# TensorE's merged order planned with measured durations, and a minimum stay on dense tiles

## The chip, the cores and the metric

One core of a Trainium2 chip runs the kernel. The metric is the device time of one execution in microseconds (us), lower is better; the kernel before takes 3297.18 us (median of 3 runs, 3290.95 to 3297.7).

## What is computed

One inference step of a two-layer hybrid decoder, for a prompt of 1024 positions and 8 decode rows. Cut to what matters:

```python
def hybrid_layer(x, ...):                       # D = 1024, 8 attention heads, 8 RWKV heads of 64
    p = x @ w_in                                # dense: in-projection
    att = dilated_attention(rope(q), rope(k), v)            # three patterns, merged
    z = token_shift(p[..., ATT_COLS:], ...)
    rw = rwkv7_time_mix(z)                      # a scan over positions: state S carried on
    x1 = layer_norm(ALPHA * x + concat(att, rw) @ w_out)    # dense: out-projection
    return layer_norm(ALPHA * x1 + square(relu(x1 @ w_ff_up)) @ w_ff_down)  # dense: feed-forward
```

Two layers run one after the other; the state of the RWKV scan, the keys and the decode rows are results too.

## The kernel before

Positions are split into two halves of 512, so the dense work is four passes (l, h): layer l, half h. A dense product is split into three matmuls (high*high, high*low, low*high parts in fp32r: L370, L371, L372), 128 output rows by 512 columns (half 0) or by 256 and 264 to 272 columns (half 1). The weights are loaded, split by ScalarE and VectorE (L343, L344) and used once per pass.

All the rest of TensorE's work is small: `stage1` and `stage2` of the RWKV scan in units of 256 positions (32 units in all), attention, the transposes of `post_stream`, and the decode rows (`decode`, and `kv_stream` for their attention). Most of it runs on tiles of the array smaller than 128x128: `pl` (L1189), `pT` and `pX` (L1283), `pPQ` (L1323), `pO` (L1340, L1345, L1359) and `pz` (L1366). Each unit of stage 2 is a chain of some 16 such blocks; between two of them VectorE or ScalarE takes the result out of PSUM and makes the next operand.

TensorE's order is written at build time by the class `Streams`. Six generators (`s2`, `s1`, `att`, `post`, `kv`, `dense`, in that priority) yield steps with a modelled cost on TensorE, a modelled latency until the stream's next step is ready (multiplied by `SLK`: 1.2 in a stream's first pass, 2.2 later) and a PSUM bank's hold time. `run` steps a model clock: the first stream in priority that is ready goes next, so that dense matmuls fill what is left. `ahead` holds a stream back that is far ahead of the dense one, by the shares of `WORK` done. The engine executes its instructions in exactly this order and waits where an operand is late.

The dense stream itself waits at four places for the other streams: `Mix.wait` before each out-projection, which asks for the last unit of stage 2, the attention and, for half 1, `dec` and `kv` of that pass. The last of the four is reached inside pass (1, 0), in group 5 of the feed-forward, just ahead of the column means of a layer norm (`lnc`, L711): all of pass (1, 1)'s small work has to stand ahead of it in TensorE's order. `decode` for layer 1 is a chain behind the transpose `pdv` (L1258): DMA out and in, then four rounds of loading a piece of the state, updating it on VectorE and GpSimd and storing it (L1654 to L1665), then a DMA out and in again (L1669, L1672) and three small blocks on TensorE, `pdy` (L1676), `pdm` (L1680) and `pdq` (L1685).

Five stretches of the program are named here by those waits: A, up to the first out-projection's wait; B, C and D, up to the second, third and fourth; E, the rest, in which only dense work is left.

Of the kernel before, what the change touches and what calls it, by code (L numbers as in the profile page):

```python
# [42 lines left out]
ALT0 = 2500  # L43
ALT1 = 4
WORK = {"s2": (73e3, 74e3, 73e3, 74e3), "s1": (38e3, 42e3, 42e3, 45e3), "att": (29e3, 49e3, 29e3, 49e3),
        "dense": (519e3, 536e3, 382e3, 394e3)}
SLK = (1.2, 2.2)
PACE = 2.0
LEAD = 0.25
# [95 lines left out]
class Streams:  # L145
# [5 lines left out]

    def __init__(self, depth):
        self.now = 0.0
        self.depth = depth
        self.hist = {b: [] for b in depth}
        self.streams = []
        self.times = {}
        self.cost = {}  # L160
        self.phase = {}
        self.work = {}

    def add(self, name, gen, slack=(1.0, 1.0)):
        self.streams.append([name, gen, 0.0, None, None, slack])
# [56 lines left out]
    def run(self):  # L222
        while self.streams:
            best = None
            main = self.ready(self.streams[-1])
            for s in self.streams:
                t = self.ready(s)
                if t is None:
                    continue
                if main is not None and main <= self.now and s is not self.streams[-1] and self.ahead(s):  # L230
                    continue
                if t <= self.now:
                    best = (t, s)
                    break
                if best is None or t < best[0]:
                    best = (t, s)
            assert best is not None, [s[0] for s in self.streams]
            self.now = max(self.now, best[0])
            self.step(best[1])


def bc(ap, dims):
# [5 lines left out]
def body(ctx, tc, I, O):  # L248
# [17 lines left out]
    def bank(tag, name):  # L266
        return ps.tile([128, 512], F32, tag=tag, bufs=BANKS[tag], name=name)
# [93 lines left out]
    def dense_steps(items, kts, xhh, xll, res):  # L361

        pts = [bank("d", "dps") for _ in items]
        last = len(kts) - 1
        for i, (wk, kt) in enumerate(kts):
            cost = 0
            for p, (w, m, c0, n) in zip(pts, items):
                wh, wl = w[wk // 4]
                hi, lo = xhh(kt, c0, n), xll(kt, c0, n)
                PE.matmul(p[:m, :n], wh[:, wk % 4, :m], hi, start=(i == 0), stop=False)  # L370
                PE.matmul(p[:m, :n], wh[:, wk % 4, :m], lo, start=False, stop=False)  # L371
                PE.matmul(p[:m, :n], wl[:, wk % 4, :m], hi, start=False, stop=(i == last))  # L372
                cost += 3 * (n / 2.4 + 2.5)
            if i < last:
                yield (cost, None, 0, None)
        res += pts
        res.append(cost)

    def dense(items, kts, xhh, xll, evac):

        res = []
        yield (0, None, 0, "d")
        yield from dense_steps(items, kts, xhh, xll, res)
        for it, p in zip(items, res):
            r = evac(it, p)
            if r is not None:
                yield r
        for i, it in enumerate(items):
            yield (res[-1] if i == 0 else 0, ("d", 900 + 500 * i), 0, None)
# [1468 lines left out]
```

## Time and profile before

| | |
|---|---|
| median of 3 runs | 3297.18 us |
| profiled execution, its own time | 3297.23 us |
| its span, first to last instruction | 3295.4 us |
| TensorE matmul busy | 3148.5 us, 96%, 24732 instructions |
| VectorE, ScalarE, GpSimd busy | 2065.4, 1449.2, 985.1 us |
| mean granted TensorE clock | 0.983 of full speed |

TensorE is the busiest engine by far. Matmuls overlap in the pipeline, so a matmul's duration is longer than its pitch: what counts is the distance from one start to the next. Time in which TensorE is not busy is a wait, and the granted clock tells how much of the busy time ran at half speed.

### The profile page before, as it was taken

Reading aid. Unit: us, or ns where it says so; the run is one execution under the profiler, and the core shown is the slowest. Engines: PE = TensorE matmul, PEld = TensorE weight load, DVE = VectorE, ACT = ScalarE, POOL = GpSimd, SP = SyncE. Lnnn points to the kernel's source line nnn. Section 1 sums busy time; section 2 is a strip of 40 time slices with the busy share of each in tenths; the row PEclk is TensorE's granted clock in tenths of the full one; section 3 lists DMA queues with packets and bytes.
Section 4 is the critical chain, followed back from the end, with each engine's and each line's share of the span. In section 5 each row is a group of like instructions: output and inputs, shape, how many; then the busy total and the mean of one; then the engine's idle time right before and its main releaser. Section 6 shows DMA issues by size and latency. Waiting matters only on the chain. (4 is left out here: it accounts for less than half of the span.)

```text
span 3295.4 us, 65986 instructions
## 1 busy us (share of the span) xinstructions
PE 3148.5 (96%) x24732; PEld 2656.9 (81%) x24732; DVE 2065.4 (63%) x4703; ACT 1449.2 (44%) x3266; POOL 985.1 (30%) x1841
## 2 busy tenths in 40 slices
PE   9899999999999999989999999999999999899998
PEld 6668887776777787778999998877766778899997
DVE  4566566865555575687655566568765564875556
ACT  4455344543443364454444346445543333543334
POOL 2452436522112234452221022545321201520012
PEclk9999999999999999999999999999999999999999
DMA  7544545334433355532333235553443433423332
GB/s 229 149 136 127 147 123 154 102 114 137 118 94 95 91 157 166 175 89 87 104 96 86 81 91 171 155 157 98 122 132 108 118 93 102 133 81 93 92 90 83
DMA packets 370502, 393.57 MB, mean 119 GB/s; under 512 B 145816, under 2 KB 223080, under 8 KB 370184
## 3 DMA queue, kind: packets, MB, share of 16 engines
q10 hardware_dynamic: 121152, 213.44, 21.9%
q1 hardware_dynamic: 249032, 175.93, 18.7%
q8 instruction: 195, 3.19, 0.4%
q14 instruction: 123, 1.01, 0.1%
HBM read 325.30 MB, written 63.97 MB: 118 GB/s over the span
## 5 line engine op out<-in xcount | busy, mean ns | idle before, releaser
L370 PE MATMUL dps<-xh,wh 128*128 128x256 f32 (+3 forms) x2984 | 991.9, 332 | 18.6 <-ACT wh L343 8.1
L371 PE MATMUL dps<-xl,wh 128*128 128x256 f32 (+3 forms) x2984 | 945.5, 317 | 7.8 <-DVE xl L762 6.3
L372 PE MATMUL dps<-xh,wl 128*128 128x256 f32 (+3 forms) x2984 | 944.0, 316 | 1.7 <-DVE wl L344 1.5
L343 ACT CAST wh<-wr 128x512 fp32r<-128x512 f32 (+1 forms) x772 | 475.3, 616 | 842.4 <-PE dps L371 780.1
L344 DVE TENSOR_TENSOR wl<-wr,wh 128x512 fp32r<-128x512 f32 (+1 forms) x772 | 578.1, 750 | 348.6 <-ACT wh L343 334.3
L370 PEld LDWEIGHTS dps<-xh,wh 128*128 128x128 f32 x2984 | 566.1, 190 | 90.8 <-issue 26.7
L371 PEld LDWEIGHTS dps<-xl,wh 128*128 128x128 f32 x2984 | 566.9, 190 | 42.3 <-DVE xl L762 9.8
L372 PEld LDWEIGHTS dps<-xh,wl 128*128 128x128 f32 x2984 | 566.3, 190 | 40.5 <-DVE wl L344 3.9
L370 PE MATMUL dps<-hh,wh 128*128 128x512 f32 (+2 forms) x1600 | 535.7, 335 | 5.0 <-DVE hh L944 3.6
L371 PE MATMUL dps<-hl,wh 128*128 128x512 f32 (+2 forms) x1600 | 512.7, 320 | 4.0 <-DVE hl L833 2.8
L372 PE MATMUL dps<-hh,wl 128*128 128x512 f32 (+2 forms) x1600 | 511.9, 320 | 0.0
L370 PEld LDWEIGHTS dps<-hh,wh 128*128 128x128 f32 x1600 | 303.6, 190 | 44.2 <-issue 17.9
L372 PEld LDWEIGHTS dps<-hh,wl 128*128 128x128 f32 x1600 | 303.9, 190 | 22.4
L371 PEld LDWEIGHTS dps<-hl,wh 128*128 128x128 f32 x1600 | 304.2, 190 | 22.1 <-DVE hl L833 3.8
L1212 POOL TENSOR_TENSOR tm<-BL,XB 32x15 f32<-32x15 f32 (+7 forms) x480 | 155.4, 324 | 491.6 <-DMA BL<-d_el 406.4
L976 DVE TENSOR_TENSOR t<-dps,t 128x256 f32<-128x256 f32 (+1 forms) x240 | 123.5, 515 | 161.5 <-PE dps L372 161.0
L1214 POOL TENSOR_TENSOR XB<-XB,tm 32x15 f32<-32x15 f32 (+7 forms) x480 | 157.9, 329 | 34.1
L729 POOL TENSOR_TENSOR ln<-ln,lsq 128x256 f32<-128x256 f32 (+1 forms) x112 | 93.4, 834 | 235.0 <-ACT lsq L727 232.0
L944 DVE CAST hh<-rl 128x256 fp32r<-128x256 f32 (+2 forms) x200 | 73.4, 367 | 99.2 <-ACT rl L943 95.9
L718 POOL TENSOR_TENSOR t<-t,ln 128x256 f32<-128x256 f32 (+1 forms) x32 | 28.0, 914 | 351.8 <-ACT ln L712 351.8
L942 ACT ACTIVATE rl<-dps 128x256 f32<-128x256 f32 (+2 forms) x200 | 88.4, 442 | 99.3 <-PE dps L372 87.4
L370 PE MATMUL dps<-hh,xh 128*128 128x256 f32 (+1 forms) x368 | 113.2, 307 | 15.4 <-DVE t L933 6.3
(345 smaller groups left out, 5072.0 us busy)
## 6 DMA issues: line engine op xcount, KB each, us to landing
wr<-in_w_ff_up ACTq DMA_DIRECT2D x272, 256.0 KB
wr<-in_w_ff_down ACTq DMA_DIRECT2D x256, 256.0 KB
wr<-in_w_in ACTq DMA_DIRECT2D x220, 256.0 KB
stg<-d_qkv SPq DMA_DIRECT2D x128, 128.0 KB
wr<-in_w_out ACTq DMA_DIRECT2D x64, 256.0 KB
z<-d_z SPq DMA_DIRECT2D x24, 384.0 KB
d_qkv<-qe SPq DMA_DIRECT2D x128, 64.0 KB
kvc<-in_cache_k SPq DMA_DIRECT2D x32, 256.0 KB
```

The costliest lines, as they stand in the source:

```text
L343: self.copies.append(A.copy(h[:, :, :m], w[:, :, :m]))
L344: V.tensor_tensor(lo[:, :, :m], w[:, :, :m], h.bitcast(F32)[:, :, :m], op=ALU.subtract)
L370: PE.matmul(p[:m, :n], wh[:, wk % 4, :m], hi, start=(i == 0), stop=False)
L371: PE.matmul(p[:m, :n], wh[:, wk % 4, :m], lo, start=False, stop=False)
L372: PE.matmul(p[:m, :n], wl[:, wk % 4, :m], hi, start=False, stop=(i == last))
L718: G.tensor_tensor(t, t, self.cm[:, c0:c0 + n], op=ALU.subtract)
L729: G.tensor_tensor(s2, s2, sq, op=ALU.add)
L942: A.activation(r, p[:, :n], AF.Relu)
L944: V.tensor_copy(hh[:, c0:c0 + n], r)
L976: V.tensor_tensor(to, p[:, :n], to, op=ALU.add)
L1212: G.tensor_tensor(tv, bc(BL[:, 17 * j + 1:17 * j + 2], [(1, m), (0, j + 1)]), bc(XB[:, 16 * j:16 * j + 1], [(0, m), (1, j + 1)]), op=ALU.mult)
L1214: G.tensor_tensor(xv, xv, tv, op=ALU.add)
```

## The change

The cost of a dense matmul of n columns in the model goes from n/2.4 + 2.5 ns to 0.447 n + 4 ns, and the dense entries of `WORK` go up by the same 8%. Each time the order comes back to the dense stream after a step of another stream that took TensorE time, the model clock goes on by `SWITCH` = 280 ns. From the point on at which the dense stream has entered its first out-projection, such a return also sets `stay`: for the next `RUN` = 3200 ns of the model clock the dense stream goes on as long as the model has it ready, whatever else is ready. No instruction is added or removed; the order of TensorE's instructions changes, and with it that of the other engines and of the DMA queues, which the scheduler derives.

```diff
-        "dense": (519e3, 536e3, 382e3, 394e3)}
+        "dense": (561e3, 580e3, 413e3, 427e3)}
+RUN = 3200
+SWITCH = 280
...
     def __init__(self, depth):
...
+        self.stay = 0.0
+        self.away = False
...
     def run(self):
         while self.streams:
             best = None
-            main = self.ready(self.streams[-1])
+            last = self.streams[-1]
+            main = self.ready(last)
+            free = main is not None and main <= self.now
+            if free and self.now < self.stay:
+                self.step(last)
+                continue
             for s in self.streams:
                 t = self.ready(s)
                 if t is None:
                     continue
-                if main is not None and main <= self.now and s is not self.streams[-1] and self.ahead(s):
+                if free and s is not last and self.ahead(s):
                     continue
...
             self.now = max(self.now, best[0])
-            self.step(best[1])
+            if best[1] is not last:
+                at = self.now
+                self.step(best[1])
+                self.away |= self.now > at
+                continue
+            if self.away:
+                self.away = False
+                self.now += SWITCH
+                if "dense" in self.phase:
+                    self.stay = self.now + RUN
+            self.step(last)
...
-                cost += 3 * (n / 2.4 + 2.5)
+                cost += 3 * (0.447 * n + 4)
```

Lines behind the change stand 20 further down in the changed kernel (L370 is L390 there).

TensorE, end of stretch D, in the order before: the decode block `pdq` (`cst` holds constants, `a` the decode rows) stands among the dense matmuls of the feed-forward.

```order
L371 MATMUL dps<-xl_90,wh 128x512
L372 MATMUL dps<-xh_88,wl 128x512
L1685 MATMUL pdq<-a,cst 128x32
L370 MATMUL dps<-xh_88,wh 128x512
L371 MATMUL dps<-xl_90,wh 128x512
```

Between `pdv` and `pdq` there are 339 dense matmuls, and 138 more between `pdq` and the first `lnc`. The same place in the changed order, from the last blocks of the last unit of stage 2 on:

```order
L1386 MATMUL pz<-cst,St 64x64 x2
L1399 MATMUL pzf<-cst,Zp 64x64 x2
L1400 MATMUL pzf<-gs,gup 128x8
L1407 MATMUL pgm<-y,cst 128x256
L1408 MATMUL pgm<-gs,gup 128x256
L1416 MATMUL pgv<-gq,cst 128x256
L1696 MATMUL pdy<-cst,dyr 128x8 x4
L1700 MATMUL pdm<-a,cst 128x32
L1705 MATMUL pdq<-a,cst 128x32
L731 MATMUL lnc<-t,onec 128x256 x2
L390 MATMUL dps<-xh_88,wh 128x512
```

Only 21 dense matmuls are left between `pdv` and `pdq`, all of them close behind `pdv`, and none between `pdq` and `lnc`: the end of unit 30, the whole of unit 31, the last attention and the decode blocks stand in one row without a dense matmul among them.

TensorE, stretch A, the second unit of stage 1, from `pl` to the transposes `pt` of the same unit, before:

```order
L1189 MATMUL pl_981<-AR,BK 128x128
L1189 MATMUL pl_982<-AR,BK 128x128
L370 MATMUL dps<-xh_88,wh 128x512
L371 MATMUL dps<-xl_90,wh 128x512
L372 MATMUL dps<-xh_88,wl 128x512
L370 MATMUL dps<-xh_89,wh 128x512
L371 MATMUL dps<-xl_91,wh 128x512
L372 MATMUL dps<-xh_89,wl 128x512
L1231 MATMUL pt_1051<-cst,BK 128x128 x4
```

and with the change:

```order
L1209 MATMUL pl_918<-AR,BK 128x128
L1209 MATMUL pl_919<-AR,BK 128x128
L390 MATMUL dps<-xh_89,wh 128x512
L391 MATMUL dps<-xl_91,wh 128x512
L392 MATMUL dps<-xh_89,wl 128x512
L1251 MATMUL pt_1013<-cst,BK 128x128 x4
```

Three dense matmuls stand between the two blocks where there were six.

Counted over the whole order, stretches of dense matmuls go from 762 to 581, and the times that TensorE comes from a 128x128 tile (dense or not) to a smaller one from 552 to 517: 125 to 139 in stretch A, 162 to 139 in B, 126 to 122 in C, 139 to 117 in D.

## Rows read from the trace of the kernel before

**Rows 1.** The page: busy time by engine, and TensorE's granted clock in 40 slices.

```profile
PE 3148.5 (96%) x24732; PEld 2656.9 (81%) x24732; DVE 2065.4 (63%) x4703; ACT 1449.2 (44%) x3266; POOL 985.1 (30%) x1841
...
PEclk9999999999999999999999999999999999999999
```

**Rows 2.** Windows A to E: stretch, length, busy by engine (instructions), PEclk, DMA share, GB/s.

```profile
0.00:499.00 499.00, 475.02 (x3929) 384.96 (x3931) 302.51 (x805) 239.05 (x560) 185.72 (x394) 0.99 0.52 152
499.00:1356.40 857.40, 819.59 (x5837) 636.13 (x5834) 531.82 (x1193) 372.35 (x837) 274.84 (x544) 0.98 0.43 124
1356.40:2168.60 812.20, 781.98 (x6870) 718.19 (x6869) 521.28 (x1214) 371.63 (x858) 246.63 (x458) 0.99 0.39 113
2168.60:2737.40 568.80, 546.91 (x4143) 413.43 (x4142) 366.46 (x851) 242.74 (x556) 162.37 (x319) 0.98 0.40 116
2737.40:3295.40 558.00, 524.98 (x3962) 504.22 (x3960) 343.34 (x642) 223.47 (x457) 115.52 (x129) 0.97 0.32 96
```

**Rows 3.** TensorE's waits, stretches B to D: who waited for whom, total us, times, longest.

```profile
PE pz L1366 <- DVE St L1361: 9.1, 4, 2.7
PE dps L370 <- DVE t L933: 6.3, 2, 4.5
...
PE pS L1552 <- DVE bv L1250: 0.2, 1, 0.2
```

**Rows 4.** Timeline of TensorE: start us, us, engine, line, operation, tiles, shape, count.

```profile
871.02 0.40 PE L372 MATMUL dps<-hh,wl 128*128 128x512 f32 x1
871.35 0.33 PE L1366 MATMUL pz<-cst,St 64*64 64x64 f32 x4
871.61 1.16 PE L1189 MATMUL pl<-AR,BK 64*128 64x128 f32 x16
...
873.04 0.39 PE L371 MATMUL dps<-hl,wh 128*128 128x512 f32 x1
...
1012.57 0.39 PE L372 MATMUL dps<-hh,wl 128*128 128x512 f32 x1
1012.89 1.16 PE L1189 MATMUL pl<-AR,BK 64*128 64x128 f32 x16
...
1014.32 0.40 PE L371 MATMUL dps<-xl,wh 128*128 128x512 f32 x1
1014.55 0.40 PE L372 MATMUL dps<-xh,wl 128*128 128x512 f32 x1
1014.88 0.33 PE L1366 MATMUL pz<-cst,St 64*64 64x64 f32 x4
...
1015.48 0.40 PE L371 MATMUL dps<-xl,wh 128*128 128x512 f32 x1
```

**Rows 5.** TensorE's waits, stretch A.

```profile
PE pO L1359 <- DVE Z L1368: 4.3, 2, 3.9
PE pt L1231 <- DVE LB L1194: 4.2, 2, 2.2
```

**Rows 6.** Source line L1194: count, duration ns min/median/max, first and last start.

```profile
L1194 DVE TENSOR_TENSOR LB<-pl,cst x128: 405/414/426, 64.1 to 2591.3; 128x256 f32<-128x256 f32 x128
```

**Rows 7.** Timeline of TensorE: decode of layer 0 (first row) and layer 1, and `lnc`.

```profile
1027.57 0.29 PE L1258 MATMUL pdv<-cst,dvt 128*40 128x128 f32 x1
...
2604.02 0.27 PE L1258 MATMUL pdv<-cst,dvt 128*40 128x128 f32 x1
...
2699.98 0.41 PE L1676 MATMUL pdy<-cst,dyr 8*128 8x8 f32 x4
...
2707.36 0.30 PE L1685 MATMUL pdq<-a,cst 128*128 128x32 f32 x2
...
2739.51 1.02 PE L711 MATMUL lnc<-t,onec 128*128 128x256 f32 x4
```

**Rows 8.** Source line L1672: the last DMA in of each layer's decode, first and last start.

```profile
L1672 SPq DMA_DIRECT2D dyr<-d_y x2: 297/300/302, 1100.1 to 2673.5; - x2
```

**Rows 9.** Timeline of VectorE: the first of four rounds of layer 1's decode.

```profile
2618.07 0.69 DVE L1655 TENSOR_TENSOR dt<-ST,DV 128x512 f32<-128x512 f32 x1 [3.10 <-DMA DV<-d_dec]
```

## The prediction

> **What bounds the kernel now.** I read the page first: TensorE is busy for 3148.5 of 3295.4 us, the next engine for 2065.4, and the clock row is nearly full everywhere [rows 1]. So the time is TensorE's work plus its waits plus what a lower clock costs; a change of order leaves the work itself as it is. Then the windows by stretch, to place the waits: length less busy is 24.0 us in A, 37.8 in B, 30.2 in C, 21.9 in D and 33.0 in E [rows 2], 147 in all. The clock column says what ran at half speed: (1 - 0.98) * 857 = 17 us lost in B, 0.01 * 812 = 8 in C, 0.02 * 569 = 11 in D, 36 together. Then the waits by name for B to D: 41 rows, of which [rows 3] shows the first two and the last; 37 us are waits of dense matmuls and of the layer norm's blocks, which the change does not aim at, and 52 us are waits of the small blocks, the largest of them `pz` for `St`: a chain step whose operand was not ready when its turn in the order came. The profiled execution took 3297.23 us, against a median of 3297.18, so a difference worked out on it is one on the median too; about 0.2%, 6.6 us, is what a measurement of this kernel can tell from no change.
>
> **The change, term by term.**
>
> *Fewer comings and goings.* In [rows 4] a matmul of 512 columns takes 0.23 us from start to start (1014.32 to 1014.55). Around `pz` alone, from the last dense start before it to the second one after it, it takes 1015.48 - 1014.55 = 0.93, less two pitches 0.46. Around `pl` alone it is 1014.32 - 1012.57 - 0.47 = 1.28. Around both in one row it is 873.04 - 871.02 - 0.47 = 1.55, where 0.46 + 1.28 = 1.74 would be the sum. So putting two blocks of small tiles side by side saves 0.19 us, not the 0.28 that the model now charges for each return. What counts by this is how often TensorE comes from a 128x128 tile to a smaller one: 35 times fewer, at 0.2 us 7 us saved; by stretch, A has 14 more (2.8 us lost) and B, C and D have 49 fewer (9.8 us gained; 7 that follow at the end of D are counted in). The ends are nothing and 181 stretches fewer at 0.2, 36 us, if every avoided return saved as much; I keep 7, since many of the blocks that now stand together are a small tile beside a full one, for which I take no saving.
>
> The Trainium skill, TensorEngine Tiling (Array Packing), Key Properties, says that changing the tiling mode, and not just the tile, drains TensorE. By it a row of `pz` (64*64) and `pl` (64*128) would drain as well between the two and save nothing, and the sum below would be 7 us higher. The rows contradict that for this pair by 0.19 us, and I follow the rows.
>
> *Chains in B to D.* By the order and the pitch, the TensorE work between a `pO` and the next `pz` goes from 2.2 to 2.8 us to 3.3 to 4.4 us, since the stay keeps dense matmuls there for 3.2 us; the longer links, some 3.6 to 4.3 us before, change little. A wait like `pz`'s, 9.1 us in 4 times and 2.7 at most [rows 3], is then mostly covered. The gain lies between 10 us, where new waits arise as more blocks end at once and VectorE has to serve them together, and all 52. I take 28, a little over half: the short links go, the long ones, DMA waits and attention stay in part. With them goes part of the 36 us of the clock; half of it stands behind waits of small blocks, and half of that is 9 us (ends 0 and 20).
>
> *Stretch A.* Here nothing stays, the slack is 1.2, and the model's time passes faster per dense matmul, so fewer of them stand between two steps: three instead of six between `pl` and `pt` in the second unit, 0.70 us instead of 1.40, and about 1.1 instead of 1.4 between `pO` and `pz`. Four operations `LB` of 0.41 us [rows 6] lie behind `pl`, and `pt` needs a bank that the first two free, 0.83 us: what was covered is now just short, and where VectorE comes late the whole difference is paid. `pt` and `pO` already waited 4.2 and 4.3 us in two places each [rows 5]. Stretch A has some 8 units with about 16 links; 0.3 us paid on a fifth of these 130 would be 8 us. I take 9 with the clock (ends 0, as median links keep a margin, and 26, when two thirds pay).
>
> *The end of stretch D.* This is the largest term. TensorE takes its instructions in order, and behind the last of the 21 dense matmuls that follow `pdv` the order holds only small blocks until `pdq`; then come `lnc` and the dense work. So nothing dense can run until layer 1's decode has come through. How long that takes is in the trace. `pdv` started at 2604.02 [rows 7], the first of four rounds at 2618.07 [rows 9], the last DMA in was issued at 2673.5 [rows 8]: 69.5 us of DMA and VectorE work, with no dependence on dense matmuls. In layer 0 it is 1100.1 - 1027.57 = 72.5 us [rows 7, 8]. With an estimate of 3.1 us for that DMA to land (VectorE sat idle that long for the one of `DV` [rows 9]) and those 2707.36 - 2699.98 = 7.4 us [rows 7], `pdq` comes 80 us behind `pdv`. Before, 339 dense matmuls stood in that gap, 339 * 0.233 = 79 us, and 138 more, 32 us, between `pdq` and `lnc` at 2739.51 [rows 7]: all of it covered, with 32 us to spare. Now 21 * 0.233 = 4.9 us of dense work and 2.6 of small blocks lie behind `pdv`, so TensorE is without dense work for 80 - 7.5 = 72 us. In it stand the small blocks themselves: before, `pdv` to `pdq` took 103.3 us, of which 79 were dense, so the blocks of units 30 and 31 and their waits are 24; without the waits, and with the attention and `pdo` blocks that now come here too, I count 20 us of work. 72 - 20 = 52 us of waiting, and 3 more for dense matmuls that restart at the half clock: 55 us lost. The ends are 42, where the decode's DMAs get through 10 us sooner with the queue to themselves and the second load of `DV` is not held as it was before 2618.07, and 65, where VectorE's queue, now with unit 31's steps between the rounds, holds the rounds up. Unit 31's own waits of before are part of the 28, since they now lie inside this hole.
>
> *Sum:* 55 + 2.8 + 9 - 9.8 - 28 - 9 = +20 us, 3297.2 + 20 = 3317 us. Stretch E has no small work and keeps its order.
>
> **The rivals.**
>
> *The chains repay it (faster).* If the longer distances take away nearly all waits of small blocks, 45 of 52 us and 18 of the clock's 36, while the decode comes through at its short end (44 us) and A pays 3 with its entries: 44 + 3 - 45 - 18 - 9.8 = -26, 3271 us. For it: the links that waited most are those that become longest. Against it: `pz`, the largest of these waits, is 9.1 of the 52 us, and much of the rest lies on links that change less. It decides from the point at which the gains in B to D pass 58 us together.
>
> *A draw.* Both at half way: the end of D at 47, B to D gaining 47: 3297 us, within 6 us of before. Nothing speaks against it but the sizes.
>
> *Bunching (slower still).* In a burst after each stay up to four streams issue at once; two PSUM banks serve stage 1, attention and the decode rows, and VectorE at 63% [rows 1] takes their results together. If the new waits eat the 28 and 9, and A pays 20: 55 + 2.8 + 20 - 9.8 = +68, but then part of the bunches hides in the end of D; I put it at 3355.
>
> *The change does little.* That the model's stay is cut short because the model sees no dense step ready is excluded by the order itself: 338 of the 581 stretches are now 3.2 to 4 us long by the pitch, where 51 of 762 were.
>
> **How the numbers follow.** Forecast, slower by 7 to 45 us: 0.48. Bunching 0.10. Draw 0.18. Faster 0.24. The time is that of the forecast, 3317 us. The range reaches from 3276, which takes in the nearer half of the faster rival, to just below the bunching case, 3348, and leaves out about a fifth. Faster by over 0.2%: 0.24; within: 0.18; slower: 0.58.
>
> **What would show it.** In the profile after: a hole in TensorE's busy row just ahead of `lnc` in pass (1, 0), some 70 us from the last dense matmul to `lnc`, with the clock at half level and `pdy`, `pdq` waiting for the decode's DMA; waits of `pz` in B to D cut to a third; waits of `pt` and `pO` in A longer or more of them; windows B and C shorter than 857 and 812 us, D longer than 569. It is wrong if the hole is under 40 us, if A grows by over 25 us, or if B and C together shrink by over 50.

## The result and the profile after

The changed kernel takes 3342.18 us (median of 4 runs, 3337.59 to 3348.74), before on the same chip 3297.44: ratio 1.0141, 95% interval 1.0119 to 1.0163, or 45 us slower. The forecast was +20 us: the sign is right and the time lies in the stated range, but the loss is more than twice as large. The profiled execution after has a span of 3341.0 us. Two executions far from all others, one of e2 (5785.66 us) and one of the kernel before beside e9 to e12 (6189.77 us), were slow ones and are in no ratio below.

The page after, the rows that answer to [rows 1]:

```profile
PE 3160.8 (95%) x24732; PEld 2675.8 (80%) x24732; DVE 2070.7 (62%) x4703; ACT 1446.7 (43%) x3266; POOL 979.1 (29%) x1841
...
PEclk9999999999999999999999999999999988999999
```

The same instructions, and two slices of lower clock near the end of stretch D. The windows A to E after, to be read beside [rows 2]:

```profile
0.00:562.70 562.70, 512.22 (x4236) 411.07 (x4237) 326.78 (x863) 257.90 (x607) 211.23 (x471) 0.96 0.48 142
562.70:1380.40 817.70, 790.11 (x5518) 620.80 (x5516) 514.76 (x1132) 353.05 (x788) 246.36 (x465) 0.98 0.43 125
1380.40:2186.60 806.20, 779.87 (x6848) 718.26 (x6845) 510.87 (x1199) 368.44 (x852) 244.00 (x457) 0.97 0.40 114
2186.60:2782.40 595.80, 553.97 (x4187) 422.52 (x4186) 373.72 (x867) 244.37 (x563) 163.22 (x321) 0.95 0.39 113
2782.40:3341.00 558.60, 524.62 (x3954) 503.15 (x3953) 344.54 (x645) 222.95 (x458) 114.27 (x129) 0.97 0.32 95
```

A is 64 us longer, B 40 shorter, C 6 shorter, D 25 longer (cut as here, at the first `lnc`, it was 571 us). A part of A and B is only moved work: A has 4236 matmuls where it had 3929, B has 5518 where it had 5837. The waits are more than moved: in A, length less busy goes from 24.0 us to 50.5, at a clock of 0.96 in place of 0.99, while B's goes down by 10; in D it goes from 21.9 to 41.8, at 0.95.

TensorE's waits in stretch A after (who waited for whom, total us, times, longest):

```profile
PE pS L1583 <- POOL kS L1545: 9.3, 2, 6.7
PE dps L390 <- ACT wh L363: 6.6, 2, 5.3
PE pz L1386 <- DVE St L1381: 5.9, 2, 5.6
PE pO L1360 <- DVE Pt L1346: 4.3, 1, 4.3
PE pT L1303 <- DMA X<-d_el: 4.2, 3, 2.4
PE pET L1606 <- DVE E L1595: 3.4, 1, 3.4
```

Of these six, only two stood among A's waits before: `dps`, with the same 5.3 us at the start of the program, and `pz` for `St`, with 0.5 us. The new waits are few and long, not many and short. The chain behind the one of 4.3 us stands in the timeline after (start us, us, engine, line, operation; in brackets the idle time before it and what ended it):

```profile
404.29 1.09 ACT L1540 CAST qS<-stg 128x512 fp32r<-128x512 f32 x1 [5.39 <-DMA stg<-d_qkv]
...
405.28 0.61 ACT L363 CAST wh<-wr 128x512 fp32r<-128x512 f32 x1
...
405.93 1.59 DVE L364 TENSOR_TENSOR wl<-wr,wh 128x512 fp32r<-128x512 f32 x1 [3.33 <-ACT wh L363]
407.44 0.41 DVE L1346 COPY Pt<-pPQ 128x256 f32<-128x256 f32 x1
...
407.91 0.65 PE L1360 MATMUL pO<-LB,Pt 64*64 64x128 f32 x8 [4.31 <-DVE Pt L1346]
```

ScalarE sits for 5.39 us on the load of the attention's `stg` (it makes `qS` from it); the split of a dense weight (`wh`) is queued behind that, VectorE's half of the split (`wl`) waits for `wh`, and `Pt`, the operand of the scan, is queued behind `wl`. Three engines stop for one load. The waits of `pS` (`kS` is made from `stg`, and stands in GpSimd's queue as well) and `pET` lead back to `stg` too: with `pO` 17.0 us of A's waits.

The end of D after, timeline of TensorE, then the window of the hole:

```profile
2718.25 0.29 PE L1278 MATMUL pdv<-cst,dvt 128*40 128x128 f32 x1
...
2725.62 0.40 PE L392 MATMUL dps<-hh,wl 128*128 128x512 f32 x1
...
2779.93 0.59 PE L1696 MATMUL pdy<-cst,dyr 8*128 8x8 f32 x4 [2.57 <-DMA dyr<-d_y]
...
2781.98 0.64 PE L1705 MATMUL pdq<-a,cst 128*128 128x32 f32 x2 [0.54 <-ACT a L1702]
2782.43 2.05 PE L731 MATMUL lnc<-t,onec 128*128 128x256 f32 x4
```

```profile
2725.60:2782.40 56.80, 30.16 (x283) 20.07 (x282) 31.18 (x68) 8.13 (x23) 9.78 (x8) 0.59 0.33 95
```

The hole is there, from the last dense matmul to `lnc`: 56.8 us, 30.2 of them busy at a clock of 0.59.

**An account of the 45 us.** For each profiled execution I take, up to the last instruction, TensorE's idle time, half of its busy time at the half clock (1.2 of 2.4 GHz), and the dense matmuls at their pitch (0.233 us for 512 columns, as in [rows 4]); what is left over is the small blocks with all that coming and going costs. From before to after: idle time 136.0 to 169.3, clock 47.7 to 77.3, small blocks 857.6 to 840.3: +33, +30 and -17. (The level of 857.6 hangs on the pitch taken for the dense matmuls; the difference does not.)

### The profile page after: what moved, and what is told of

Its sections match the earlier page's. It is cut to its first block, busy times and chain, and to the rows that moved or that the text cites. A ratio compares the mean times of both kernels' runs of the same rounds, so it can differ in the third digit from the quotient of the medians.

```text
span 3341.0 us, 66018 instructions
## 1 busy us (share of the span) xinstructions
PE 3160.8 (95%) x24732; PEld 2675.8 (80%) x24732; DVE 2070.7 (62%) x4703; ACT 1446.7 (43%) x3266; POOL 979.1 (29%) x1841
## 5 line engine op out<-in xcount | busy, mean ns | idle before, releaser
L390 PE MATMUL dps<-xh,wh 128*128 128x256 f32 (+3 forms) x2984 | 985.9, 330 | 22.6 <-ACT xh L781 8.0
L390 PEld LDWEIGHTS dps<-xh,wh 128*128 128x128 f32 x2984 | 568.5, 191 | 93.4 <-issue 26.1
L390 PE MATMUL dps<-hh,wh 128*128 128x512 f32 (+2 forms) x1600 | 528.3, 330 | 5.2 <-DVE hh L964 3.6
L390 PEld LDWEIGHTS dps<-hh,wh 128*128 128x128 f32 x1600 | 304.9, 191 | 39.2 <-issue 11.3
L1232 POOL TENSOR_TENSOR tm<-BL,XB 32x15 f32<-32x15 f32 (+7 forms) x480 | 147.5, 307 | 571.1 <-DMA BL<-d_el 513.4
L390 PE MATMUL dps<-hh,xh 128*128 128x256 f32 (+1 forms) x368 | 110.0, 299 | 8.6 <-DVE t L1029 4.3
```

Source lines behind the costliest of these rows:

```text
L1232: G.tensor_tensor(tv, bc(BL[:, 17 * j + 1:17 * j + 2], [(1, m), (0, j + 1)]), bc(XB[:, 16 * j:16 * j + 1], [(0, m), (1, j + 1)]), op=ALU.mult)
```

## The experiments

A link is one step of a chain: the operand that VectorE or ScalarE makes, and the TensorE work that the order puts into that time. Its distance is that work; a link is too short when the next block's turn comes before its operand. Theory 1, before the first runs: the loss has two places, stretch A, where the charge makes the links too short at a slack of 1.2, and the hole at the end of D, which the stay opens. Its rivals: the bunching by the stay; the queue order of the other engines or the work moved into A, given back there; later, that any order other than that of before loses, whichever way the distances go.

Idle time of TensorE and length of the stretches, in us (cut at the same dense matmuls in all; for before within 3 us of [rows 2]), and the ratio to before. A loss in us is, from here on, that ratio applied to before's time on the same chip; for the changed kernel it gives +46.

| kernel | A | B | C | D | ratio, 95% |
|---|---|---|---|---|---|
| before | 24 of 498 | 38 of 858 | 30 of 812 | 22 of 571 | |
| after | 51 of 563 | 28 of 818 | 26 of 806 | 42 of 596 | 1.0141 (1.0119 to 1.0163) |
| e1 costs only | 27 of 510 | 49 of 873 | 31 of 815 | 21 of 563 | 1.0064 (1.0049 to 1.0079) |
| e2 costs, charge | 50 of 568 | 40 of 849 | 41 of 840 | 40 of 567 | 1.0255 (1.0236 to 1.0274) |
| e3 stay only | 24 of 497 | 47 of 849 | 25 of 807 | 46 of 605 | 1.0071 (1.0056 to 1.0086) |
| e4 after, no stay in D | 51 of 564 | 26 of 815 | 25 of 803 | 38 of 603 | 1.0137 (1.0114 to 1.0160) |
| e5 before, slack 0.85 in A | 53 of 554 | 29 of 842 | 30 of 816 | 21 of 569 | 1.0100 (1.0085 to 1.0115) |
| e6 after, charge late | 30 of 518 | 42 of 855 | 31 of 814 | 42 of 595 | 1.0118 (1.0101 to 1.0134) |
| e7 after, slack 1.6 in A | 30 of 518 | 43 of 853 | 31 of 814 | 46 of 597 | 1.0100 (1.0085 to 1.0115) |
| e8 stay only, not in D | 27 of 499 | 45 of 850 | 27 of 810 | 29 of 587 | 0.9993 (0.9982 to 1.0004) |
| e9 before, slack 1.5 in A | 24 of 479 | 40 of 882 | 30 of 809 | 23 of 577 | 1.0003 (0.9988 to 1.0017) |
| e10 before, slack 2.45 later | 25 of 498 | 43 of 869 | 24 of 807 | 27 of 580 | 1.0032 (1.0018 to 1.0046) |
| e11 before, slack 1.7 later | 26 of 512 | 46 of 871 | 26 of 823 | 29 of 550 | 1.0066 (1.0044 to 1.0088) |
| e12 costs, slacks raised | 29 of 502 | 38 of 862 | 25 of 805 | 27 of 586 | 1.0026 (1.0009 to 1.0043) |
| e13 after, stay ends in D | 52 of 565 | 27 of 819 | 27 of 806 | 25 of 575 | 1.0065 (1.0049 to 1.0080) |
| e14 e13 with slack 1.6 | 29 of 513 | 39 of 849 | 30 of 812 | 25 of 572 | 1.0031 (1.0017 to 1.0045) |
| e15 stay only, ends in D | 24 of 496 | 47 of 851 | 24 of 805 | 28 of 586 | 1.0002 (0.9990 to 1.0014) |
| e16 stay of 1600 only | 28 of 503 | 41 of 859 | 30 of 812 | 27 of 577 | 1.0019 (1.0009 to 1.0029) |
| e17 old costs, charge late | 26 of 502 | 41 of 848 | 37 of 823 | 19 of 574 | 1.0039 (1.0024 to 1.0053) |
| e18 stay only, slack 2.0 | 29 of 504 | 48 of 863 | 24 of 794 | 30 of 590 | 1.0035 (1.0022 to 1.0048) |

### The parts of the change alone (e1, e2, e3)

e1, the costs alone:

```diff
-SWITCH = 280
+SWITCH = 0
...
-                if "dense" in self.phase:
-                    self.stay = self.now + RUN
```

> Only the dense costs (0.447 n + 4 ns and the 8% in WORK); no charge per return, no stay. Theory 1 (the loss has two places: the 280 ns charge in stretch A, where the slack is 1.2, and the hole that the stay opens at the end of D): neither is here, A stays at 499 us within 12, between pdv and pdq 321 dense matmuls stand, so no hole; 3290 to 3310 us. Theory 2 (the costs themselves shorten the distances in A, since the model's time passes 8% faster per dense matmul): A grows by 20 us or more, 3315 us or more.

Measured +21 us (3317.28). The time lies in theory 2's range, A (12 us longer) in theory 1's; what neither had is B, 15 us longer, with 12 us more waits. A reading of this is that the old durations, 8% too low, had given each link 8% of distance for nothing; e12 below bears it out for 12 of the 21 us.

e2, the costs and the charge (only the two lines on `stay` taken out):

> Costs and the 280 ns charge per return, no stay. Theory 1: A comes out as in the changed kernel, 563 us within 8 with some 50 us of idle TensorE, and D has no hole (276 dense matmuls between pdv and pdq); the charge shortens the links in B to D too, where the slack of 2.2 leaves room; 3320 to 3345 us. Rival (bunching by the stay is what costs, the charge alone is harmless): 3290 to 3305 us, A within 10 us of 499.

Measured +84 us (3381.53, the median of the three executions that count), more than either theory. A is that of the changed kernel, as theory 1 has it; C is 28 us longer than before and D waits 18 us more, which I had not expected under a slack of 2.2. The windows A, B and C of this kernel:

```profile
0.00:568.10 568.10, 517.84 (x4236) 415.40 (x4237) 328.18 (x863) 258.59 (x607) 211.21 (x471) 0.95 0.48 140
568.10:1417.10 849.00, 809.04 (x5656) 633.63 (x5654) 525.05 (x1159) 366.64 (x816) 256.95 (x474) 0.98 0.44 124
1417.10:2257.00 839.90, 798.49 (x7037) 726.05 (x7034) 529.56 (x1254) 376.20 (x873) 246.38 (x458) 0.97 0.39 110
```

In the changed kernel the stay gives the distance back: B and C wait 28 and 26 us there, 40 and 41 here. So the charge costs 63 us more than the costs, and the stay repays 38 of that.

e3, the stay alone:

```diff
-        "dense": (561e3, 580e3, 413e3, 427e3)}
+        "dense": (519e3, 536e3, 382e3, 394e3)}
-SWITCH = 280
+SWITCH = 0
...
-                cost += 3 * (0.447 * n + 4)
+                cost += 3 * (n / 2.4 + 2.5)
```

> Only the stay of 3200 ns, with the old costs and no charge. Stretch A's order is that of before up to the first out-projection. Theory 1: A 499 us within 5; between the last pdv and pdq there is no dense matmul at all, so the hole ahead of lnc is there, 55 to 65 us long, 40 of it lost; B and C gain 10 to 20 us; in all 3310 to 3330 us. Rival (the loss of the changed kernel is the charge's, in every stretch, and the stay repays its hole by the chains in B to D): 3285 to 3300 us. Bunching: B and C grow, 3335 us or more.

Measured +23 us (3319.51): theory 1, but with a longer hole. A as before, B and C 14 us shorter, D 34 longer with a hole of 80.9 us (expected 55 to 65), 44.7 us of it lost: 32.3 idle and 12.4 of clock. B alone waits more than before, 47 us in place of 38.

This run also bears on what a return costs. 170 stretches of dense matmuls fewer than before (592 of 762) go with small blocks 16.3 us shorter (857.6 to 841.3), e16's 80 fewer with 7.4 us, the changed kernel's 181 fewer with 17.3: 0.10, 0.09 and 0.10 us each, where the model charges 0.28. It is an average, not a price: the other kernels with a stay give 0.07 to 0.16 us each, and e10, with 56 stretches more than before, has its small blocks 1.3 us shorter, not longer. Counted instead by the tiles in the traces' rows, TensorE comes from a 128*128 tile to a smaller one 63, 27 and 63 times less in e3, e16 and the changed kernel, and 0.26 to 0.28 us for each of these fits as well.

### Stretch A (e5, e6, e7, e9)

e5, the kernel before with shorter links in A by another route:

```diff
-SLK = (1.2, 2.2)
+SLK = (0.85, 2.2)
```

> The kernel before with one number changed: the first pass's slack 0.85 in place of 1.2, no charge, no stay, old costs. In stretch A as many dense matmuls then stand between pl and pt (median 3 in place of 6), pO and pz (mean 5.6, before 8.1) and pgm and pgv (9.4, before 15.9) as in the changed kernel or fewer. Theory 1 (A's loss is that small blocks' turns come before their operands): A grows like the changed kernel's, 545 to 580 us with 45 to 60 us of idle TensorE, and the total 3325 to 3350 us. Rival (A's loss is the queue order of the other engines that the charge brings, or the small work that moves from B into A and is given back there): A within 20 us of 498 apart from moved work, total within 10 us of before.

Measured +33 us (3336.34), A 554 us with 52.7 idle: theory 1. Windows A and B of this run, and its longest wait of a small block in A, the same as after:

```profile
0.00:554.00 554.00, 501.35 (x4087) 402.16 (x4088) 311.17 (x831) 251.70 (x588) 197.46 (x434) 0.96 0.50 141
554.00:1395.70 841.70, 812.88 (x5677) 634.99 (x5677) 518.78 (x1169) 365.61 (x810) 255.98 (x505) 0.97 0.44 124
```

```profile
PE pS L1563 <- POOL kS L1525: 8.3, 2, 5.0
```

B waits 28.8 us here, before 37.8, with no stay in this kernel: part of B's small work has moved into A (matmuls in A from 3929 to 4087, in B from 5837 to 5677), as it has in the changed kernel.

e9 goes the other way (`SLK = (1.5, 2.2)` in the kernel before):

> The kernel before with the first pass's slack 1.5 in place of 1.2, the opposite of the run with 0.85: in stretch A more dense matmuls stand between pT and pX (mean 12.4, before 9.6) and pO and pz (9.8, before 8.1). Theory 1 (distance: a small block that comes too early waits): A's waits do not grow, 24 us or fewer, A 490 to 500 us, total 3285 to 3300 us. Rival (any other order loses: the operands that come late are those that a queue of VectorE, ScalarE or GpSimd happens to hold up, in each order others): A 510 us or more, total 3310 us or more.

Measured +1 us (3303.03, 3 us above theory 1's range; before on that chip 3300.75), A's waits 23.6 us: longer links cost nothing there, though they gain nothing either. A is shorter than expected, 479 us, because small work moved to B. How ScalarE waits for `stg` in A follows the distance. Before, after, and e9 (total us, times, longest):

```profile
ACT kS L1524 <- DMA stg<-d_qkv: 18.5, 8, 4.7
ACT qS L1520 <- DMA stg<-d_qkv: 6.3, 4, 2.4
```

```profile
ACT qS L1540 <- DMA stg<-d_qkv: 16.6, 9, 5.4
ACT kS L1544 <- DMA stg<-d_qkv: 15.8, 8, 7.6
```

```profile
ACT kS L1524 <- DMA stg<-d_qkv: 9.9, 7, 2.6
ACT qS L1520 <- DMA stg<-d_qkv: 2.4, 2, 2.2
```

24.8, 32.4 and 12.3 us; with e5 it is 35.3. TensorE waits no less in e9 than before, though, so ScalarE's waits are not themselves the price. As I read it, before they lay under dense work, and with short links a step of the scan stands behind them, as in the chain shown above.

e6 charges the 280 ns only once `"dense" in self.phase`; e7 raises the slack of the changed kernel's first pass (`SLK = (1.6, 2.2)`).

> The changed kernel, but the 280 ns are charged only from the first out-projection on; in A only the higher costs are left. Theory 1: A comes back to 505 to 515 us, B takes some of the moved work back and is 825 to 850 us, C and D stay as in the changed kernel (D with its hole); 3305 to 3325 us. Rival (what A loses is gained in B): 3335 us or more.

> The changed kernel with 1.6 in place of 1.2 as the first pass's slack: the links of A have their dense matmuls back (pl to pt 6, pT to pX 10), with the charge kept. Theory 1: waits of A back to 24 to 32 us, A 500 to 520 us, total 3300 to 3320 us. Rival (the charge's order of the other engines is at fault, not the distance): A stays at 545 us or more.

Both have A back at 518 us with 30 idle, near theory 1 (e6's A is just above its range), but the totals are +39 and +33, above theory 1's ranges; e6, at 3339.91, is on its rival's side, by which what A loses is gained in B. B waits 42 and 43 us where the changed kernel waits 28. Of the 45 us that A comes back, 35 to 37 return in B, as the work that had moved into A and as waits. Net, A and B together are 1356 us before, 1380 after, and 1372 and 1371 here: repairing A is worth 8 to 13 us, not the 45 that A alone shows. The hole in these two kernels:

```profile
2724.90:2781.50 56.60, 30.19 (x284) 20.13 (x282) 31.24 (x68) 8.10 (x23) 9.78 (x8) 0.59 0.35 93
```

```profile
2722.20:2781.60 59.40, 28.81 (x299) 19.45 (x298) 31.18 (x69) 7.99 (x23) 9.78 (x8) 0.69 0.38 100
```

Outside it, B to D wait 88 and 90 us, and before 90: with A repaired, the changed kernel waits no less there than the kernel before.

### The end of stretch D (e3, e4, e8, e13, e15)

e4, the changed kernel without the stay in D:

```diff
-                if "dense" in self.phase:
+                if self.phase.get("dense", (2,))[0] != 2:
```

> The changed kernel, but without the stay while the third out-projection's pass is running (stretch D); 291 dense matmuls stand between pdv and pdq. Theory 1: the hole goes, and with it its 40 us of lost busy time and its half clock, while A keeps its loss: 3300 to 3315 us, D 555 to 570 us. Rival (the hole's time comes back as waits of unit 30's and 31's links spread over D): 3330 us or more, D 585 or more with as much idle TensorE as in the changed kernel.

Measured +45 us (3339.66), the rival's side. There is no hole, and D waits 38 us, nearly as long as with it (42). The first rows of its waits in D:

```profile
PE pT L1303 <- DMA X<-d_el: 6.6, 2, 5.8
PE dps L391 <- DVE xl L782: 6.5, 4, 3.4
PE pS L1572 <- DVE dT L1280: 4.9, 1, 4.9
```

The longest of them (5.8, 4.9 and 3.4 us) lie between 2316 and 2355 us, in the first third of D, some 370 us ahead of where the hole was. The edit changed the order of all of D, so this run did not test the hole. e8 makes the same edit to e3, e13 to e15 the cleaner one, which keeps D's order up to unit 29:

```diff
-                if "dense" in self.phase:
+                if "dense" in self.phase and (self.phase["dense"][0] != 2 or self.share("dense") < 0.5):
```

> Only the stay, with the old costs and no charge, and not while stretch D runs; 342 dense matmuls stand between pdv and pdq, so there is no hole. Theory 1, corrected by the run without the stay in D: A 497, B 849 and C 807 us as with the stay alone; D is 571 us within 10 if its loss there was the hole, so 3275 to 3290 us, faster than before. Rival (D loses by single late operands wherever its order is changed, as the run without the stay in D showed 38 us of idle TensorE without a hole): D 590 us or more, 3305 us or more.

> The changed kernel, but the stay ends when half of stretch D's dense work is done; 267 dense matmuls then stand between pdv and pdq (21 in the changed kernel), and the order up to unit 29 is that of the changed kernel. If the hole's 39 us of idle time and half clock are its own: D 570 to 582 us, total 3315 to 3330 us. Rival (unit 30's and 31's links find late operands wherever they stand): D 590 us or more, 3335 us or more.

> Only the stay, old costs, no charge, and it ends when two fifths of stretch D's dense work are done; 168 dense matmuls stand between pdv and pdq, so half of the hole is left at most. A and B 1345, C 807 as with the stay alone; D 575 to 588 us if the hole goes with its cover (605 with the stay throughout): 3285 to 3302 us. Rival (new late operands in D): D 595 or more, 3310 us or more.

Windows of stretch D, one after the other: with the stay (e3), e4, e8 and e13:

```profile
2152.70:2757.60 604.90, 558.98 (x4232) 426.66 (x4232) 371.67 (x871) 247.76 (x569) 164.29 (x320) 0.96 0.39 110
```

```profile
2181.80:2784.60 602.80, 564.98 (x4187) 426.50 (x4186) 370.60 (x872) 244.89 (x565) 161.88 (x321) 0.95 0.39 111
```

```profile
2158.90:2746.20 587.30, 558.46 (x4234) 421.49 (x4233) 374.77 (x875) 246.69 (x571) 164.20 (x320) 0.97 0.40 113
```

```profile
2190.00:2764.50 574.50, 549.98 (x4187) 416.68 (x4186) 366.56 (x865) 244.32 (x563) 162.73 (x320) 0.98 0.42 116
```

e13 shows it: D 575 us in place of 596, +21 us in all (3321.59) in place of +46, waits 24.5 in place of 41.8. Taking the hole away is worth 21 us in the window and 25 by the ratios. With the old costs (e8, e15, bound 0.4 instead of 0.5) D falls from 605 to 587 and 586, and the total from +23 to -2 and +1 us: faster than e3 by about what the hole cost in e13, but no faster than before. e8 lies between theory and rival, with D at 587; e15 in its theory's range.

### Distance in B to D (e10, e11, e12) and mixes (e14, e16, e17, e18)

The kernel before with `SLK = (1.2, 2.45)` and `(1.2, 1.7)`, and e1 with `(1.35, 2.5)`:

> The kernel before with 2.45 in place of 2.2 as the slack of the later passes; 336 dense matmuls still stand between pdv and pdq. A's order is as before up to the first out-projection. Theory 1 (distance): B, C and D keep their waits or lose some, 75 to 92 us together (before 90), total 3285 to 3302 us, with the 56 returns that there are more costing up to 10. Rival (any other order loses): 105 us of waits or more in B to D, 3315 us or more.

> The kernel before with 1.7 in place of 2.2 as the slack of the later passes, the counterpart of the run with 2.45; A's order is as before up to the first out-projection. Theory 1 (distance): waits of small blocks in B to D grow as they did in A with 0.85, from 90 to 115 us or more with a lower clock behind them, total 3320 to 3360 us. Rival (any other order loses, about as much in either direction): the same loss within 10 us as the run with 2.45.

> The new dense costs alone, no charge and no stay, with the slacks raised to 1.35 and 2.5 so that the 8% are given back and a little more: the distances are those of before or longer in A (pT to pX 10.9, before 9.6), close to before in B to D. Theory 1: the 21 us that the costs alone lost go, 3285 to 3305 us, B's waits 38 to 42 us (49 with the costs alone). Rival (any other order loses): 3312 us or more.

Measured +11, +22 and +9 us. Shorter links lose about twice what longer ones do, and giving the 8% back takes away 12 of the costs' 21 us, which speaks for distance in B to D too. It is weaker evidence than in A: e11's B to D wait 101 us in its profile (the fastest of its executions, 10 us under the median), where theory 1 asked for 115, and e10 and e12 lie above theory 1's ranges, though by less than the rival asks: waits in B to D are 94 and 90 us, as before, and the clock costs 10 and 9 us more in the whole kernel. With e11, A was not as before (512 us): streams of the second pass run ahead into it.

e14 is e13 with `SLK = (1.6, 2.2)`; e16 is e3 with `RUN = 1600`; e17 is e13 with the old costs and the charge only from the first out-projection on; e18 is e3 with `SLK = (1.2, 2.0)` and the stay ending at a share of 0.3 in D.

> The same with the first pass's slack at 1.6. The two places are repaired together: A and B were 1371 us together with that slack (changed kernel 1380, before 1356), so 8 us less than the run without it, 3305 to 3322 us; what is then left over before stands in A and B. Rival as there: 3325 us or more.

> Only a stay of 1600 ns in place of 3200, old costs, no charge: 80 returns fewer than before (170 fewer with 3200), 357 dense matmuls between pdv and pdq, no hole. If a return avoided is worth 0.1 us or a little less and links that become longer do no harm: 3283 to 3297 us. Rival (any other order than before's loses some 10 us to operands that come late elsewhere): 3300 to 3315 us.

> Old costs, the charge only from the first out-projection on, the stay until half of stretch D's dense work: A's order is that of before (498 us). If B's waits are as with the charge (39 to 43 us of idle TensorE), C and D as in the run with both repairs (812 and 572): 3280 to 3296 us. Rival (as with the stay alone, B 47 us idle, D 586): 3297 to 3312 us.

> Old costs, no charge, the stay until three tenths of stretch D's dense work, and 2.0 in place of 2.2 as the later passes' slack: 294 dense matmuls stand between pdv and pdq, no hole. If the stay itself keeps the links long enough, the shorter slack costs nothing and D is 571 to 578 us: 3285 to 3300 us. Rival (links shorter again, as with 1.7: 11 us more waits in B to D): 3305 us or more.

Measured +10, +6, +13 and +12 us. e14 repairs both places of the changed kernel and takes away 36 of the 46 us that the ratios show. Its windows A and B (its profiled execution is 7 us under its median):

```profile
0.00:513.00 513.00, 484.23 (x4027) 390.87 (x4028) 310.29 (x830) 249.61 (x589) 199.72 (x428) 0.99 0.53 151
513.00:1362.20 849.20, 809.82 (x5724) 635.71 (x5723) 529.83 (x1164) 359.92 (x805) 263.57 (x509) 0.97 0.44 123
```

e16 to e18 went the way of their rivals: their small blocks are 7 to 9 us shorter, but TensorE waits 11 to 18 us more, on operands that come late in other places (e17: C at 823 us, expected 812). No kernel of the 18 is faster than before; e8, e9 and e15 cannot be told from it.

## Why the prediction was right in sign and wrong in size

By its own terms, with the account above (waits and half clock together where the term had both):

| term | forecast | measured |
|---|---|---|
| hole at the end of D | +55 (42 to 65) | +38.5: 26.6 idle, 11.9 clock |
| A, waits and clock | +9 (0 to 26) | +39.2 (29.1 to 68.3) |
| B, C, D without the hole, waits | -28 (10 to 52) | -20.8 (89.9 to 69.1) |
| the same, clock | -9 (0 to 20) | +3.7 (33.4 to 37.1) |
| returns | +2.8 - 9.8 = -7 | -17.3 |
| E, waits and clock | 0 | +2.1 |
| sum | +20 | +45.4 (spans: +45.6) |

**The step that failed is stretch A:** "0.3 us paid on a fifth of these 130 would be 8 us". The mechanism is right (links too short at a slack of 1.2; e5 makes it without charge or costs, e6 and e7 take it away), the size is not. I had taken a missing 0.3 us as the price, because I compared the distance with the link's own operations, `LB` at 0.41 us [rows 6]. What is paid is set by whatever stands ahead in the queue of the engine that makes the operand: a load of `stg` for `pS`, `pO` and `pET`, worth 2.6 to 6.7 us at a time, and a long VectorE instruction for `pz`. Five waits over 3 us (`pS`, `pz`, `pO`, `pET` and the start's `dps`) are 25 of A's 50 us; the last stood before too, so the four new ones are 20 of the 26.5 us added. The half clock behind such waits adds 12.7 us (5.1 to 17.8). The wrong-if condition "A grows by over 25 us" came true. Net of what B gets back, repairing A is worth 8 to 13 us (e6, e7; e14 against e13: 11), near the 9 forecast; that is luck, as neither A's own loss nor B's share in it was foreseen.

**The hole** was forecast by its right mechanism and over-sized by 15 us: 56.8 us in place of 72. `pdv` to `pdq` took 63.7 us, not 80. The last DMA in was issued at 2778.3, 60.0 behind `pdv`, where the trace of before had 69.5 and 72.5 [rows 7, 8]; `pdy` started 1.6 us behind that, not 3.1; and `pdy` to `pdq` took 2.05 us in place of 7.4 [rows 7], as no dense matmuls stand between them. Its price of 38.5 us is below the end of 42: 26.6 us of waiting where I had 52, and 11.9 of lower clock where I had 3. The 20 us of small work in it were right: 30.2 busy less 11.9 of lower clock is 18.3. e13 gives back 21 to 25 of the 38.5. Of the rest, 9 us are waits that D has without a hole (24.5 us where the changed kernel has 15.2 outside its own), 3 its clock and 4 the small blocks, with 40 stretches more.

**Chains in B to D** are the second step that failed: the sum credits 28 us of waits and 9 of clock to the stay, and adds A as a separate term. By the account B to D wait 21 us less, but the runs do not show that this is the stay's. e5, without a stay, waits 80 us in B to D in place of 90, and e6, e7 and e14, with the stay and A repaired, 88, 90 and 94 outside the hole. Against e2, which has the same costs and charge, the stay does gain (81 to 54 us in B and C), but once A is repaired that does not lead below the 68 us of before (72, 74 and 70 in e6, e7 and e14; 73 with the stay alone, e3). So A's loss and B's gain are in part one thing, small work moved from B into A; the chains did not repay the hole, and the faster rival (58 us together) was far off. The clock did not gain: in C, 19 waits of blocks other than the dense ones, of 0.8 us on average, became 7 of 1.4, so what went was short and what stayed was long. **Bunching** did not come: B and C wait less than before, in e4 as well. **Returns** were under-sized: I counted 35 net entries to smaller tiles at 0.2 us, and the small blocks became 17 us shorter. Whether that goes by the 181 stretches fewer (0.10 us each) or by the 63 entries fewer that the traces show (600 to 537, 0.27 us each) the runs do not separate. The drain on a mode change that the Trainium skill states (TensorEngine Tiling (Array Packing), Key Properties) may be what is saved there, but no run here separates modes from either count.

What stays open is the 10 us that e14 still loses, and e10, e12, e16, e17 and e18 with it. By size it could be one wait of 10.6 us in D of e14, described below; an order without that wait was not tried, and the lower clock costs 13 us more in B and C of e14 than before.

## What to carry to other kernels

Before making a model's durations truer, ask what its errors were doing: here 8% too little per dense matmul and no price per return acted as distance in disguise, and raising the slack with them gave a part back (12 of 21 us in e12, 11 in e14). The price of a step that came early was here not its own shortfall but the longest thing queued ahead on the engine that feeds it, so look along that queue for a load or a burst. Before adding up stretches as separate terms, ask whether work can move between them: what A lost and B gained was in good part the same work. And a minimum stay for the filler needed an end here: behind the last pass the filler has to be kept for the longest chain that is still to come.

## What was not expected of the hardware

The longest wait of the changed kernel, 8.9 us of `pO` in D, stands behind one VectorE instruction. Timeline after, VectorE, then GpSimd, then TensorE:

```profile
2249.57 11.63 DVE L1595 TENSOR_SCALAR E<-E,mx 128x640 f32<-128x640 f32 x1
...
2262.93 0.27 DVE L1388 TENSOR_SCALAR Z<-pz,Wd 128x64 f32<-128x64 f32 x1
...
2250.19 6.92 POOL L738 TENSOR_TENSOR t<-t,lnm 128x256 f32<-128x256 f32 x10
...
2259.60 1.25 POOL L1545 TENSOR_TENSOR kS<-stg,kS 64x512 fp32r<-64x512 f32 x1
...
2263.25 0.69 PE L1379 MATMUL pO<-FG,Z 64*64 64x128 f32 x4 [8.92 <-DVE Z L1388]
```

An instruction that otherwise takes 0.55 us stands for 11.63, from 2249.57 to 2261.20, while GpSimd runs without a gap until 2260.85, ten operations of a layer norm's `shift` among its work. It is no single case. In the traces of before, after, e4, e8 and e13, 45 VectorE instructions stand for over 1.5 us longer than usual, and GpSimd is busy for 97 to 100% of the time of 42 of them (76, 88 and 93% for the other three). The wait of `pz` in A (5.6 us, a subtraction of two tiles, L819, that took 6.33 us in place of 0.70), one of 10.7 us in D of e13 (behind a split of a dense weight that took 7.41 us) and one of 10.6 in D of e14 (behind the same `E`, 13.34 us) are of this kind. In all five kernels with the new costs, the charge and the stay in D's first half (after, e6, e7, e13, e14) this `pO` waits 8.9 to 10.7 us, 76 to 78 us into D. The Trainium skill (SBUF — State Buffer, SBUF: two separate sides) says that VectorE operations with two SBUF inputs or in a two-port mode and GpSimd operations share a port that one of them holds for a whole instruction while the other is blocked. The trace fits this, as VectorE stands for 11.63 us beside a busy GpSimd; it goes further in that VectorE did not get in between GpSimd's instructions, ten and more in a row. No run takes GpSimd's work away, so that the port is the cause is not shown here. The VectorE time beyond the usual durations is the same in both orders (175 us before and after, counting excesses over 0.3 us); whether a link of the scan stands behind such an instruction differs.
